# A batched matmul with 24 KB weight runs, half-lane ends and the x cast moved to VectorE

## The chip, the cores and the metric

One core of one Trainium2 chip runs the kernel; the chip's other cores are idle. The metric is the device time of one execution in microseconds (us). A timed comparison is several runs of a kernel and of the kernel before on the same chip. Ratios are the mean time of one kernel's fast runs over that of the other's of the same rounds, so they are not quite the ratio of the medians that are quoted.

## The reference

128 independent products, each [256 x 512] times [512 x 384] in fp32:

```python
b1, b2, m, k, n = 8, 16, 256, 512, 384
x      = randn(b1, b2, m, k)      # 67 MB
weight = randn(b1, b2, k, n)      # 101 MB
out    = np.matmul(x, weight)     # 50 MB
```

## The kernel before

Four products make a group, so there are 32 groups. A group's x lies in 128 partitions of eight rows (16 KB runs), its output the same way (12 KB runs). The kernel casts x and weights to bf16 and transposes x on TensorE. Then it multiplies, with each strip of 32 output partitions serving one of the four products. A lane is one of a tile's partitions, 128 of them in most tiles (the x cast's form on the page is 128x1024); PSUM is where the code puts TensorE's results, the tiles `pt` and `po`. A packet is one partition's run: the page counts 18,864, which is 128 for each of the 131 transfers and 16 of 4 bytes for its semaphore, 9 ns each. In the code the semaphores count work done, and `wait_ge` holds an engine until a count is reached (SyncE is held 269.5 us by casts of weights, in the waits view).

```python
G = 4; R = 8; T = 4; D = 2; S = 2; HP = 64      # group of 4, two pairs, halves of 64 lanes
XS, WS, OS = 2, 4, 4                            # buffers of x, of weight pairs, of output
BS, TS, WBS = 1, 2, 8                           # x in bf16, x transposed, weights in bf16

def load(e, t, U, s):                           # SyncE: two weight pairs, then x
    for d in range(G // D):
        e.wait_ge(w_cast, ...)                  # this buffer's old weights are cast
        e.dma_start(w_sb[slot][:], ...)         # 128 runs of 12 KB
    e.wait_ge(x_cast, ...)
    e.dma_start(x_sb[s % XS][:], ...)           # 128 runs of 16 KB

def prepare(e, t, U, s):                        # VectorE
    for d in range(G // D):
        ...                                     # wait for the pair
        for a in range(D):
            for h in range(S):
                e.tensor_copy(w_bf[...][h*HP:(h+1)*HP], w_sb[slot][a*HP:(a+1)*HP, ...])
    for q in range(T):
        e.wait_ge(t_made, ...)
        e.tensor_copy(x_t[...], pt[...])        # transposed x, PSUM to SBUF

def multiply(e, t, U, s):                       # TensorE: transposes of group n, then its products
    for q in range(T):
        e.wait_ge(x_cast, ...)
        ...                                     # 4 transposes
    e.wait_ge(w_cast, ...)
    for q in range(T):
        ...                                     # 32 matmuls
# ScalarE: four casts of x (cast_x), then four copies of the products to out_sb (copy_out)
# SyncE's loop: load group n, then store group n - 4
... (cut)
```

Of the kernel before, what the change touches and what calls it, by code (L numbers as in the profile page):

```python
# [12 lines left out]
def kernel(  # L13
# [6 lines left out]
    nc = tc.nc  # L20
    P = 128

    b1, b2, M, K = x.shape
    _, _, _, N = weight.shape
    B = b1 * b2
    KO = K // P

    x_rows = x.rearrange("b1 b2 m k -> (b1 b2 m) k")
    w_rows = weight.rearrange("b1 b2 k n -> (b1 b2 k) n")
    o_rows = out.rearrange("b1 b2 m n -> (b1 b2 m) n")  # L30

    fp32 = mybir.dt.float32
    bf16 = mybir.dt.bfloat16
# [3 lines left out]



    G = 4  # L40
    C = P // G
    R = G * M // P
    T = R // 2
    D = 2
    S = 2
    HP = P // D
    NG = B // G

    XS, WS, OS = 2, 2 * G // D, 4
    BS, TS, WBS = 1, 2, 2 * G  # L50
    PT, PO = 4, 2

    LAG = 4

    ctx.enter_context(tc.tile_critical(no_gpsimd_drain=True))  # L55

    def sbuf(name, shape, dtype, n):
        return [
            ctx.enter_context(nc.sbuf_tensor(f"{name}{s}", shape, dtype)) for s in range(n)
        ]  # L60
# [6 lines left out]
    def sems(name, n):  # L67
        return [tc.alloc_semaphore(f"{name}{s}") for s in range(n)]
# [2 lines left out]
    identity = sbuf("identity", [P, P], fp32, 1)[0]  # L71
    x_sb = sbuf("x_sb", [P, R, K], fp32, XS)

    x_bf = sbuf("x_bf", [P, R, S, HP, KO], bf16, BS)
    x_t = sbuf("x_t", [P, R, KO // 2, P, 2], bf16, TS)
    w_sb = sbuf("w_sb", [P, S * KO, N], fp32, WS)
    w_bf = sbuf("w_bf", [P, KO, N], bf16, WBS)
    out_sb = sbuf("out_sb", [P, R, N], fp32, OS)
    pt = psum("pt", [P, 2, KO // 2, P], fp32, PT)
# [2 lines left out]



    id_done, x_cast, w_cast, t_made, t_copied, p_made, o_copied = (
        sems(name, 1)[0]
        for name in (
            "id_done", "x_cast", "w_cast", "t_made", "t_copied", "p_made", "o_copied"
        )
    )  # L90
    x_in, w_in, o_out = sems("x_in", XS), sems("w_in", WS), sems("o_out", OS)


    BIAS = 8


    def load(e, t, U, s):
        n = t * U + s
        for d in range(G // D):
            slot = (s * (G // D) + d) % WS  # L100
            if not isinstance(n, int) or n >= 2:
                e.wait_ge(w_cast, n * (G * S) + ((d + 1) * D * S - 2 * G * S))
            e.dma_start(  # L103
                w_sb[slot][:],
                w_rows[bass.ds(n * (G * K) + d * (D * K), D * K)].rearrange(
                    "(p k) n -> p k n", k=S * KO
                ),
            ).then_inc(w_in[slot], 16)
        if not isinstance(n, int) or n >= XS:
            e.wait_ge(x_cast, n * T + (1 - XS) * T)  # L110
        e.dma_start(  # L111
            x_sb[s % XS][:],
            x_rows[bass.ds(n * (G * M), G * M)].rearrange("(p r) k -> p r k", r=R),
        ).then_inc(x_in[s % XS], 16)

    def store(e, t, U, s, pieces=1):
        n = t * U + s
        dram = o_rows[bass.ds(n * (G * M), G * M)].rearrange("(p r) n -> p r n", r=R)
        for q in range(pieces):
            rows = slice(q * R // pieces, (q + 1) * R // pieces)  # L120
            e.wait_ge(o_copied, n * T + ((q + 1) * T // pieces + BIAS))
            e.dma_start(out=dram[:, rows], in_=out_sb[s % OS][:, rows]).then_inc(
                o_out[s % OS], 16
            )

    def cast_x(e, t, U, s, q):
        n = t * U + s
        if q == 0:
            e.wait_ge(x_in[s % XS], (t * (U // XS) + s // XS) * 16 + 16)
        e.wait_ge(t_made, n * T + (q + 1 - T + BIAS))  # L130
        rows = slice(2 * q, 2 * q + 2)
        e.copy(  # L132
            out=x_bf[s % BS][:, rows],
            in_=x_sb[s % XS][:, rows].rearrange("p r (q s c) -> p r s q c", s=S, c=KO),
        ).then_inc(x_cast, 1)

    def prepare(e, t, U, s):
        n = t * U + s
        e.wait_ge(p_made, n * T + (BIAS - T))
        for d in range(G // D):  # L140
            slot = (s * (G // D) + d) % WS
            e.wait_ge(
                w_in[slot], (t * (U * G // D // WS) + s * G // D // WS) * 16 + 16
            )
            for a in range(D):
                for h in range(S):
                    e.tensor_copy(  # L147
                        out=w_bf[(s * G + d * D + a) % WBS][h * HP : (h + 1) * HP],
                        in_=w_sb[slot][a * HP : (a + 1) * HP, h * KO : (h + 1) * KO, :],
                    ).then_inc(w_cast, 1)  # L150
        for q in range(T):
            e.wait_ge(t_made, n * T + (q + 1 + BIAS))
            e.tensor_copy(  # L153
                out=x_t[s % TS][:, 2 * q : 2 * q + 2],
                in_=pt[(s * T + q) % PT][:].bitcast(bf16),
            ).then_inc(t_copied, 1)

    def multiply(e, t, U, s):
        n = t * U + s
        words = x_bf[s % BS][:].rearrange("p r s q c -> p r (s q c)").bitcast(fp32)  # L160
        for q in range(T):
            e.wait_ge(x_cast, n * T + (q + 1))
            e.wait_ge(t_copied, n * T + (q + 1 - PT + BIAS))
            for rr in range(2):
                for h in range(KO // 2):
                    ins = e.transpose(  # L166
                        pt[(s * T + q) % PT][:, rr, h, :],
                        words[:, 2 * q + rr, h :: KO // 2],
                        identity[:],
                    )  # L170
            ins.then_inc(t_made, 1)
        e.wait_ge(w_cast, n * (G * S) + G * S)
        for q in range(T):
            e.wait_ge(t_copied, n * T + (q + 1 + BIAS))
            e.wait_ge(o_copied, n * T + (q + 1 - PO + BIAS))
            for rr in range(2):
                for ko in range(KO):
                    for i in range(G):
                        mine = slice(i * C, (i + 1) * C)
                        ins = e.matmul(  # L180
                            po[(s * T + q) % PO][mine, rr, :N],
                            x_t[s % TS][:, 2 * q + rr, ko // 2, mine, ko % 2],
                            w_bf[(s * G + i) % WBS][:, ko, :],
                            start=(ko == 0),
                            stop=(ko == KO - 1),
                        )
            ins.then_inc(p_made, 1)

    def copy_out(e, t, U, s, q):
        n = t * U + s  # L190
        if q == 0:
            e.wait_ge(o_out[s % OS], (t * (U // OS) + s // OS) * 16 + 16)
        e.wait_ge(p_made, n * T + (q + 1 + BIAS))  # L193
        e.copy(  # L194
            out=out_sb[s % OS][:, 2 * q : 2 * q + 2, :],
            in_=po[(s * T + q) % PO][:, :, :N],
        ).then_inc(o_copied, 1)
# [7 lines left out]
    def on_sync(e):  # L205
        U = OS
        for n in range(LAG):
            load(e, 0, NG, n)
        rounds = (NG - LAG) // U
        with e.Fori(0, rounds) as t:  # L210
            for s in range(U):
                load(e, t, U, LAG + s)
                store(e, t, U, s)
        for n in range(rounds * U, NG):
            if n + LAG < NG:
                load(e, 0, NG, n + LAG)
            store(e, 0, NG, n, T if n == NG - 1 else 1)
        for s in range(OS):
            e.wait_ge(o_out[s], 16 + 16 * (NG // OS + (T - 1 if s == (NG - 1) % OS else 0)))

    def on_vector(e):
        U = 2
        e.sem_inc(t_copied, BIAS)
        with e.Fori(0, NG // U) as t:
            for s in range(U):
                prepare(e, t, U, s)

    def on_tensor(e):
        U = 2
        e.sem_inc(t_made, BIAS)  # L230
        e.sem_inc(p_made, BIAS)
        e.wait_ge(id_done, 2)

        pe = mybir.EngineType.PE
        with nc.Fori(0, NG // U, engines=OrderedEngineSet([pe]), head_slot={pe: 0}) as t:
            for s in range(U):
                multiply(e, t, U, s)

    def on_scalar(e):
        U = OS  # L240
        e.sem_inc(o_copied, BIAS)
        for s in range(OS):
            e.sem_inc(o_out[s], 16)

        with e.Fori(0, NG // U) as t:
            for s in range(U):
                for q in range(T):
                    cast_x(e, t, U, s, q)
                for q in range(T):
                    copy_out(e, t, U, s, q)  # L250

    on_gpsimd(nc.gpsimd)
    on_sync(nc.sync)
    on_vector(nc.vector)
    on_tensor(nc.tensor)
    on_scalar(nc.scalar)


# [28 lines left out]
```

## Time and profile before

| what | value | where |
|---|---|---|
| time | 518.8 us, median of 3, 518.78 to 518.82 | timed runs |
| moved | 218.1 MB at 429 GB/s in mid-run | queue line, windows |
| busy, VectorE / TensorE / ScalarE | 64% / 59% / 46% | page, part 1 |

How to read it: each kernel's page gives the busy time of every engine, the DMA line in 40 slices (9 means 90% or more), the chain that ended last and the groups of instructions. A row of the windows view gives the stretch, its length, the busy time of the engines asked for, TensorE's granted clock, the share of the sixteen DMA engines' time, and GB/s. The lines themselves stand in the prediction.

### The profile page before, as it was taken

The numbers are of one execution on the slowest core, as the hardware profiler recorded it, in microseconds if no ns is written. First come the engines' busy times: TensorE is split into PE (matmuls) and PEld (weight loads), VectorE is DVE, ScalarE is ACT, GpSimd is POOL, SyncE is SP. The second block draws the span as 40 slices with busy tenths as digits, with TensorE's granted clock in tenths as the row PEclk, the third lists the DMA queues.
The fourth block names the chain that finished last, engine by engine and source line by source line (L and its number), as shares of the span: only waits on it lengthen the run. The fifth ranks groups of instructions, "written<-read, shape, count | busy, mean of one in ns | idle before, by whom it ended". The sixth has DMA issues, their size and how long they took to land.

```text
span 517.2 us, 11523 instructions
## 1 busy us (share of the span) xinstructions
PE 306.6 (59%) x4608; PEld 200.6 (39%) x4608; DVE 332.8 (64%) x384; ACT 236.7 (46%) x264; POOL 0.7 (0%) x6
## 2 busy tenths in 40 slices
PE   0478776556665457645577554776446765467752
PEld 0345444334443334433344332444324443244431
DVE  3698875667556676556675566855658656676550
ACT  0465564443644436435355354454444544544441
POOL 0000000000000000000000000000000000000000
PEclk9998877878777887878777778877788877778777
DMA  8999999999999999999999999999999999999996
GB/s 340 430 423 424 424 432 426 429 428 430 432 427 427 427 428 432 429 427 430 426 431 431 426 429 430 427 432 427 427 429 429 427 433 425 430 428 430 429 428 251
DMA packets 18869, 218.18 MB, mean 422 GB/s; under 512 B 2096, under 2 KB 2096, under 8 KB 2608
## 3 DMA queue, kind: packets, MB, share of 16 engines
q1 hardware_dynamic: 18864, 218.11, 99.3%
q8 instruction: 3, 0.05, 0.0%
q14 instruction: 2, 0.02, 0.0%
HBM read 167.77 MB, written 50.33 MB: 422 GB/s over the span
## 4 chain that ended last, share of the span: by engine, by line
DMA 81%; ACT 10%; PE 4%; issue 3%; ACTq 0%; SPq 0%
DMA x_sb<-in_x_dram 81%; ACT x_bf L132 9%; PE po L180 2%; PE pt L166 1%; ACTq L130 0%; ACT out_sb L194 0%; SPq L111 0%; SPq L103 0%; ACT L132 0%; ACTq L193 0%; SPq L282 0%; SPq L55 0%
## 5 line engine op out<-in xcount | busy, mean ns | idle before, releaser
L147 DVE CAST w_bf<-w_sb 64x1536 bf16<-64x1536 f32 x256 | 244.4, 955 | 47.2 <-DMA w_sb<-in_weight_dram 38.5
L166 PE MATMUL pt<-identity,x_bf 128*128 128x128 f32 x512 | 123.7, 425 | 199.3 <-ACT x_bf L132 199.1
L180 PE MATMUL po<-w_bf,x_t 128*32 128x384 bf16 x4096 | 185.1, 342 | 1.0 <-issue 1.0
L166 PEld LDWEIGHTS pt<-identity,x_bf 128*128 128x128 f32 x512 | 91.8, 216 | 232.1 <-issue 218.3
L194 ACT COPY out_sb<-po 128x768 f32<-128x768 f32 x128 | 102.2, 798 | 147.2 <-PE po L180 147.2
L153 DVE COPY x_t<-pt 128x1024 bf16<-128x1024 bf16 x128 | 88.4, 691 | 122.3 <-PE pt L166 121.8
L132 ACT CAST x_bf<-x_sb 128x1024 bf16<-128x1024 f32 x128 | 124.4, 1042 | 80.9 <-DMA x_sb<-in_x_dram 80.8
L180 PEld LDWEIGHTS po<-w_bf,x_t 128*32 128x32 bf16 x4096 | 108.8, 101 | 73.8 <-issue 14.2
L132 ACT ACT_TABLE_LOAD x8 | 10.3, 1283 | 42.9 <-DMA x_sb<-in_x_dram 42.9
masks.py:199 POOL TENSOR_SCALAR_AFFINE_SELECT identity<-identity 128x128 f32<-128x128 f32 x1 | 0.3, 292 | 0.2 <-POOL identity L200 0.2
L200 POOL MEMSET identity<- 128x128 f32 x1 | 0.2, 204 | 0.5 <-SPq L55 0.5
L271 POOL MEMSET const-bfloat16-1.0<- 128x1 bf16 x1 | 0.1, 101 | 0.0
L271 POOL MEMSET const-uint8-127<- 128x1 uint8 x1 | 0.1, 101 | 0.0
L271 POOL MEMSET const-float32-0.0<- 128x1 f32 x1 | 0.1, 98 | 0.2 <-issue 0.2
L271 POOL MEMSET const-float32-1.0<- 128x1 f32 x1 | 0.1, 98 | 0.0
## 6 DMA issues: line engine op xcount, KB each, us to landing
w_sb<-in_weight_dram SPq DMA_DIRECT2D x64, 1536.0 KB, 27.5
x_sb<-in_x_dram SPq DMA_DIRECT2D x32, 2048.0 KB, 27.5
out_dram<-out_sb SPq DMA_DIRECT2D x31, 1536.0 KB, 30.7
out_dram<-out_sb SPq DMA_DIRECT2D x4, 384.0 KB, 5.9
```

Source lines behind the costliest of these rows:

```text
L132: e.copy(out=x_bf[s % BS][:, rows], in_=x_sb[s % XS][:, rows].rearrange("p r (q s c) -> p r s q c", s=S, c=KO),).then_inc(x_cast, 1)
L147: e.tensor_copy(out=w_bf[(s * G + d * D + a) % WBS][h * HP : (h + 1) * HP], in_=w_sb[slot][a * HP : (a + 1) * HP, h * KO : (h + 1) * KO, : ...
L153: e.tensor_copy(out=x_t[s % TS][:, 2 * q : 2 * q + 2], in_=pt[(s * T + q) % PT][:].bitcast(bf16),).then_inc(t_copied, 1)
L166: ins = e.transpose(pt[(s * T + q) % PT][:, rr, h, :], words[:, 2 * q + rr, h :: KO // 2], identity[:],)
L180: ins = e.matmul(po[(s * T + q) % PO][mine, rr, :N], x_t[s % TS][:, 2 * q + rr, ko // 2, mine, ko % 2], w_bf[(s * G + i) % WBS][:, ko, :], ...
L194: e.copy(out=out_sb[s % OS][:, 2 * q : 2 * q + 2, :], in_=po[(s * T + q) % PO][:, :, :N],).then_inc(o_copied, 1)
L200: e.memset(identity[:], 0.0).then_inc(id_done, 1)
L271: nc = _bacc.Bacc("TRN2", target_bir_lowering=False, num_devices=1)
```

## The change

It lengthens a weight load from two transfers with runs of 12 KB per partition to one with runs of 24 KB. A run of 24 KB puts a product's weights into 32 partitions, so each cast covers 32 lanes and there are 16 of them, not 8. VectorE cannot take them all: 16 and four x casts would last over the 15.9 us in which a group's bytes move. So ScalarE gets five, VectorE eleven. In exchange VectorE casts x and ScalarE copies the transposed x out of PSUM. VectorE casts the next group's x between its weight casts, and TensorE transposes it ahead of this group's products. SyncE's order changes too: it issues x, the store, then weights, where it issued weights, x, then the store. The first four groups and the last two stay with 12 KB halves and casts of 64 lanes.

```diff
-    D = 2
-    S = 2
+    SH, SL = 2, 4                     # rows of weights per partition in short and long groups
-    XS, WS, OS = 2, 2 * G // D, 4
+    XS, WS, OS = 2, 2, 4
+    CA = 5                            # weight casts of ScalarE
+    CV = G * SL - CA                  # of VectorE
+    XV = 8                            # of these, ahead of the next x
+    def is_short(n):
+        return isinstance(n, int) and (n < LAG or n >= NG - 2)
+    def load_w(e, t, U, s):           # waits for both engines' casts, then one transfer (short: two)
...
     def on_tensor(e):
+        transpose(e, 0, NG, 0)
-            for s in range(U):
-                multiply(e, t, U, s)
+            transpose(e, t, U, 1)
+            multiply(e, t, U, 0)
+            with e.If(t < NG // U - 1):
+                transpose(e, t, U, 2)
+            multiply(e, t, U, 1)
...
+        def step(t, U, s):            # VectorE
+            cast_w(e, t, U, s, range(XV))
+            next_x(t, U, s)
+            cast_w(e, t, U, s, range(XV, CV), False)
...
+        def step(t, U, s):            # ScalarE
+            evacuate(e, t, U, s + 1)
+            for q in range(T):
+                copy_out(e, t, U, s, q)
+                if q > 0:             # long groups: one cast, one, then three
+                    cast_w(e, t, U, s + 1, ...)
... (cut: semaphores, SyncE's order x, store, weights, unrolled ends)
```

## The prediction

> **What bounds the kernel now.** I read the page from the top: busy shares first, then the line of the DMA engines, then the chain that ended last, then the waits of the queue that issues the transfers, and last the two ends in windows. The busy shares, the slices and the queues:
>
> ```profile
> span 517.2 us, 11523 instructions
> ...
> PE 306.6 (59%) x4608; PEld 200.6 (39%) x4608; DVE 332.8 (64%) x384; ACT 236.7 (46%) x264; POOL 0.7 (0%) x6
> ...
> DMA  8999999999999999999999999999999999999996
> GB/s 340 430 423 424 424 432 426 429 428 430 432 427 427 427 428 432 429 427 430 426 431 431 426 429 430 427 432 427 427 429 429 427 433 425 430 428 430 429 428 251
> ...
> q1 hardware_dynamic: 18864, 218.11, 99.3%
> ```
>
> No engine is above 64%, but the one DMA queue fills 99.3% of sixteen engines' span, and between the first and the last slice nothing dips. The chain agrees, and so do the groups of instructions:
>
> ```profile
> DMA 81%; ACT 10%; PE 4%; issue 3%; ACTq 0%; SPq 0%
> ...
> L147 DVE CAST w_bf<-w_sb 64x1536 bf16<-64x1536 f32 x256 | 244.4, 955 | 47.2 <-DMA w_sb<-in_weight_dram 38.5
> ...
> L194 ACT COPY out_sb<-po 128x768 f32<-128x768 f32 x128 | 102.2, 798 | 147.2 <-PE po L180 147.2
> L153 DVE COPY x_t<-pt 128x1024 bf16<-128x1024 bf16 x128 | 88.4, 691 | 122.3 <-PE pt L166 121.8
> L132 ACT CAST x_bf<-x_sb 128x1024 bf16<-128x1024 f32 x128 | 124.4, 1042 | 80.9 <-DMA x_sb<-in_x_dram 80.8
> ```
>
> The casts wait for data from the DMA; the idle time of ScalarE and TensorE follows from that. The transfers' own waits need care:
>
> ```profile
> SPq L103 <- DVE w_bf L147: 269.5, 60, 8.6
> SPq L111 <- ACT x_bf L132: 122.5, 30, 5.6
> ```
>
> SyncE waits 269.5 + 122.5 us for buffers to come free. By itself that looks like "slow casts hold back the loads". It does not: a load takes 27.5 us from issue to landing (the page's part on DMA issues), far longer than its bytes need, so it spends most of this behind other transfers. The buffers are late, the DMA engines are not empty. The windows show how full they are:
>
> ```profile
> core 0: us, PE busy (x) PEld busy (x) DVE busy (x) ACT busy (x) POOL busy (x), PEclk, DMA share, GB/s
> ...
> 60.00:450.00 390.00, 237.01 (x3580) 154.81 (x3572) 257.50 (x297) 182.04 (x203) 0.00 (x0) 0.79 1.01 429
> ...
> 500.00:505.00 5.00, 5.00 (x96) 3.52 (x99) 2.02 (x3) 2.02 (x3) 0.00 (x0) 0.88 1.01 428
> 505.00:510.00 5.00, 1.87 (x48) 1.01 (x40) 0.00 (x0) 1.72 (x3) 0.00 (x0) 1.00 0.98 409
> 510.00:517.20 7.20, 0.00 (x0) 0.00 (x0) 0.00 (x0) 0.00 (x0) 0.00 (x0) 0.60 0.31 124
> ```
>
> A share of 1.01 (packet records overlap by some ns) at 429 GB/s over 390 us, and still 428 GB/s at 505 us, where the last group is being multiplied. So the time is bytes over rate plus two short ends. In the trace's packet records the first packet starts at 2.0 us and all engines are full until about 511 us; then they run out one after another, the last at 515.4 us. One group of four products moves 2.097 MB of x, 3.146 MB of weights and 1.573 MB of output, 6.816 MB, which at 429 GB/s is 15.9 us; 32 of them are 509 us, and the remaining 8 us of the span are the ends.
>
> [...] between 60 and 450 us a packet of 12,288 B lasts 461.3 ns on average and one of 16,384 B 614.5 ns. The 4,096 B more cost 153.1 ns; three times that is 459.4 ns, so the fixed part of a 12 KB packet is about 2 ns.
>
> [...]
>
> **The change part by part.** Bytes: none removed.
>
> (1) Runs. 26 of 32 groups load their weights as one transfer of 24 KB per partition in place of two of 12 KB; the first four and last two keep halves of 12 KB. Each long group saves 128 packets, 26 x 128 = 3328, at 2 ns each over 16 engines: 0.4 us. It also saves one transfer's 16 semaphore packets of 9 ns, one per engine: 26 x 9 ns = 0.2 us. Together 0.6 us, 0.1% of the time, all on the path. That is the entire direct gain I can find.
>
> (2) VectorE. It loses the PSUM copies of the transposed x (4 x 0.69 = 2.8 us per group) and gets the x cast: [...] about 0.69 us, four of them 2.8 us. [...] Weight casts go from 8 of 64 lanes to 16 of 32 lanes; [...] each still costs 955 ns (in the timeline eight in a row take 7.86 us, 0.98 each). VectorE keeps 11: 11 x 0.98 = 10.8 us. Sum 13.6 us per long group against 10.6 before.
>
> (3) ScalarE. It loses the x casts (4.2 us) and gets four PSUM copies of 1024 (about 1.04 us each, 4.2 us) and five weight casts of 1536 elements: [...] 1.47 us each, 7.3 us. With the output copies (4 x 0.80 = 3.2 us) that is 14.7 us per long group against 7.4 before. Whole-run busy time should be near 410 us on VectorE and 425 us on ScalarE.
>
> (4) Order on TensorE. Transposes of group n+1 go before the products of n. Now about 4 us of transposes stand between the x cast and the products; this takes them out of that chain. It shortens a group's latency, which is not what ends the kernel: worth 0.
>
> (5) Buffers. Still two of x and two of weights, so a buffer goes round in 31.8 us (two periods). Weights are now held until all casts are through, roughly 13.6 us after landing if VectorE starts at the landing, which leaves 31.8 - 13.6 = about 18 us from issue to landing, in place of 27.5. The x load stands behind that weight load on the same issuing engine; it would be issued just after it and take about 23 us to land. A load's own bytes need 4.9 to 7.3 us, so there would still be over 10 us of transfers ahead of each new one. I expect no gap.
>
> (6) Ends. The last loads are followed by the stores of groups 27 to 31, 3.7 us each. After the last weights land (halves let VectorE cast the first while the second comes) come about 4 us of casts, 5.4 us of products and a copy, some 11 us, while four older stores keep the engines busy for 4 x 3.7 = 14.7 us. So the last store should be ready in time and the tail be as before; likewise the head, where the first load is issued at once in both. Worth 0 +- 1 us.
>
> Sum: 518.8 - 0.6 = 518.2 us.
>
> **The rivals.** First, ScalarE or VectorE becomes the bound. For: 14.7 and 13.6 us of a 15.9 us period are 92% and 86%[...], and each waits on the other through TensorE. [...] Against: the rate of the weight cast and two weight buffers of slack.
>
> Second, weight buffers held too long starve the DMA queue. For: long loads free a buffer only as a whole, and only when the slower of two engines is done. Against: the 10 us computed in (5). If it did happen, a 1 us gap per group would make 544 us, so even a small gap shows.
>
> Third, longer runs lift the transfer rate itself[...]. For: the engines end 4 us apart, so the slowest sets the end. [...] Against: 16 KB packets move at 26.66 bytes per ns and 12 KB ones at 26.63; nothing rises with size. [...]
>
> **Range and chances.** The centre is 518.2 us. Repeats differ by 0.04 us; the ends can move by 1 us either way, and a mild third rival could take 1 or 2 us. The first two rivals lie above, with some 7% of passing 529 us or more. Range 516.3 to 520.4 us. Faster by over 2%[...]: 1%. Within 2%: 92%. Slower: 7%.
>
> **What would show each step.** Right: DMA share still 1.01 at 428 to 430 GB/s in mid-run; packets about 15,100; weights landing about 18 us after issue and x later; weight casts 955 ns on VectorE and 1.47 us on ScalarE; x cast on VectorE near 0.69 us; TensorE's transposes ahead of the products with the time unmoved. Wrong: a digit of 8 or less in the DMA line in mid-run, [...] ScalarE busy over 90% in the middle with the loads waiting for its casts, a 24 KB packet well off 921 ns, or a tail in which the engines stand empty before the last store is issued.

The sum came to 518.8 - 0.4 - 0.2 = 518.2 us: 2 ns a packet and 9 ns a semaphore packet both come from the packet records of the kernel before. The 0.69 us of an x cast on VectorE and the 1.47 us of a weight cast on ScalarE went into the 13.6 and 14.7 us a group and into point (5); when the forecast was made no trace showed them, and the run after does: 688 and 1468 ns. It also shows that a cast of 32 lanes lasts as long as one of 64 (951 and 955 ns on VectorE), and a PSUM copy of 1024 on ScalarE took 1025 ns. The small size of the third rival and the 1% for faster stand as estimates; that the rate had no more room was not shown.

## The result, and the profile after

518.6 us (median of 4 runs, 518.19 to 518.67) against 518.8 us; ratio 0.9994, interval 0.9977 to 1.0012. Same time, 0.4 us from the predicted 518.2 us and inside the range. From the page of the changed kernel:

```profile
span 516.8 us, 11572 instructions
...
PE 315.2 (61%) x4608; PEld 225.4 (44%) x4608; DVE 397.7 (77%) x462; ACT 410.3 (79%) x387; POOL 0.7 (0%) x6
...
q1 hardware_dynamic: 15120, 218.11, 99.0%
...
DMA 57%; DVE 29%; issue 9%; PE 1%; SPq 1%; DVEq 1%; ACT 0%
...
L162 DVE CAST w_bf<-w_sb 32x1536 bf16<-32x1536 f32 x286 | 271.9, 951 | 81.6 <-DMA w_sb<-in_weight_dram 73.5
...
L162 ACT CAST w_bf<-w_sb 32x1536 bf16<-32x1536 f32 x130 | 190.9, 1468 | 6.0 <-DMA w_sb<-in_weight_dram 2.8
...
L188 ACT COPY x_t<-pt 128x1024 bf16<-128x1024 bf16 x128 | 120.3, 1025 | 22.1 <-PE pt L201 21.5
L149 DVE CAST x_bf<-x_sb 128x1024 bf16<-128x1024 f32 x128 | 80.0, 688 | 12.4 <-DMA x_sb<-in_x_dram 11.5
...
w_sb<-in_weight_dram SPq DMA_DIRECT2D x26, 3072.0 KB, 18.1
x_sb<-in_x_dram SPq DMA_DIRECT2D x32, 2048.0 KB, 22.3
```

Every duration is near its forecast: weight casts 951 and 1468 ns, the x cast 688 ns. ScalarE has gone from 237 to 410 us, and yet the queue is as full. The chain now gives 29% to VectorE. That is no sign of a VectorE bound: the chain walks from a landing back to the cast that released the buffer. It can't see that the transfer had others ahead of it. The last figures of the two transfer lines show that it had: 18.1 and 22.3 us from issue to landing. The windows in mid-run (columns as in the prediction) show the rate up:

```profile
60.00:450.00 390.00, 244.55 (x3480) 174.80 (x3484) 312.64 (x363) 342.05 (x316) 0.00 (x0) 0.76 1.01 431
```

431 against 429 GB/s over nearly 500 us should be worth 2 us. The end of the kernels shows where that goes. First the kernel before, in windows of 1 us, with GpSimd as the only engine column (it is idle):

```profile
core 0: us, POOL busy (x), PEclk, DMA share, GB/s
...
510.00:511.00 1.00, 0.00 (x0) 1.00 1.02 412
511.00:512.00 1.00, 0.00 (x0) 0.70 0.67 270
512.00:513.00 1.00, 0.00 (x0) 0.50 0.28 111
513.00:514.00 1.00, 0.00 (x0) 0.50 0.16 65
514.00:515.00 1.00, 0.00 (x0) 0.50 0.07 28
```

And the changed kernel:

```profile
510.00:511.00 1.00, 0.00 (x0) 1.00 0.45 181
511.00:512.00 1.00, 0.00 (x0) 0.55 0.22 89
512.00:513.00 1.00, 0.00 (x0) 0.50 0.06 25
513.00:514.00 1.00, 0.00 (x0) 0.50 0.07 28
514.00:515.00 1.00, 0.00 (x0) 0.50 0.05 22
```

A share of 0.06 is one engine of sixteen. Most engines end over 1 us earlier after the change, and then one engine works alone for nearly 3 us.

The packet records can be taken further. They carry no engine number. But divided over sixteen chains, nearly every packet of the kernels before and after starts 3 to 4 ns before the end of another, and so each packet can be given to the engine whose previous one had just ended. Of 15,000 to 19,000 packets a few dozen at most (5 to 41) fit with a gap of over 60 ns; that is the quality of what follows. The end of the last store on each engine, and the profiled execution's own time:

| kernel (names as in the next section) | fastest engine | mean | last engine | time | time less last |
|---|---|---|---|---|---|
| before | 511.0 | 512.2 | 515.4 | 518.98 | 3.6 |
| changed | 509.6 | 510.8 | 514.9 | 518.58 | 3.7 |
| changed, again | 509.6 | 510.7 | 514.6 | 518.31 | 3.7 |
| split | 511.5 | 512.6 | 516.1 | 519.77 | 3.6 |
| order_only | 511.5 | 512.7 | 517.2 | 520.87 | 3.7 |

The time is the last engine's end plus 3.6 to 3.7 us in all of them; over the mean engine it lies anything from 6.8 to 8.2 us. The change brings the mean engine forward by 1.4 us, the last one by 0.5 us.

### The profile page after: what moved, and what is told of

Same layout as the page of the kernel before. It is cut to its first block, busy times and chain, and to the rows that moved or that the text cites. A ratio compares the mean times of both kernels' runs of the same rounds, so it can differ in the third digit from the quotient of the medians.

```text
span 516.8 us, 11572 instructions
## 1 busy us (share of the span) xinstructions
PE 315.2 (61%) x4608; PEld 225.4 (44%) x4608; DVE 397.7 (77%) x462; ACT 410.3 (79%) x387; POOL 0.7 (0%) x6
## 4 chain that ended last, share of the span: by engine, by line
DMA 57%; DVE 29%; issue 9%; PE 1%; SPq 1%; DVEq 1%; ACT 0%
DMA w_sb<-in_weight_dram 57%; DVE w_bf L162 20%; DVE x_bf L149 5%; DVE w_bf L178 4%; PE po L219 1%; SPq L125 0%; DVEq L288 0%; SPq L108 0%; DVEq L158 0%; ACT out_sb L233 0%; SPq L120 0%; DVEq L146 0%; DVEq L172 0%; SPq L372 0%; SPq L60 0%
## 5 line engine op out<-in xcount | busy, mean ns | idle before, releaser
L162 DVE CAST w_bf<-w_sb 32x1536 bf16<-32x1536 f32 x286 | 271.9, 951 | 81.6 <-DMA w_sb<-in_weight_dram 73.5
L219 PE MATMUL po<-w_bf,x_t 128*32 128x384 bf16 x4096 | 200.6, 359 | 38.3 <-DVE w_bf L162 21.0
L201 PE MATMUL pt<-identity,x_bf 128*128 128x128 f32 x512 | 115.0, 415 | 152.2 <-DVE x_bf L149 152.2
L162 ACT CAST w_bf<-w_sb 32x1536 bf16<-32x1536 f32 x130 | 190.9, 1468 | 6.0 <-DMA w_sb<-in_weight_dram 2.8
L201 PEld LDWEIGHTS pt<-identity,x_bf 128*128 128x128 f32 x512 | 103.4, 224 | 164.1 <-issue 163.8
L219 PEld LDWEIGHTS po<-w_bf,x_t 128*32 128x32 bf16 x4096 | 122.0, 106 | 115.9 <-issue 40.7
L188 ACT COPY x_t<-pt 128x1024 bf16<-128x1024 bf16 x128 | 120.3, 1025 | 22.1 <-PE pt L201 21.5
L149 DVE CAST x_bf<-x_sb 128x1024 bf16<-128x1024 f32 x128 | 80.0, 688 | 12.4 <-DMA x_sb<-in_x_dram 11.5
L178 DVE CAST w_bf<-w_sb 64x1536 bf16<-64x1536 f32 x48 | 45.9, 955 | 8.3 <-DMA w_sb<-in_weight_dram 7.0
## 6 DMA issues: line engine op xcount, KB each, us to landing
w_sb<-in_weight_dram SPq DMA_DIRECT2D x26, 3072.0 KB, 18.1
x_sb<-in_x_dram SPq DMA_DIRECT2D x32, 2048.0 KB, 22.3
```

The costliest lines, as they stand in the source:

```text
L149: e.tensor_copy(out=x_bf[s % BS][:, rows].rearrange("p r (s q c) -> p r s q c", s=S, c=KO), in_=x_sb[s % XS][:, rows].rearrange("p r (q s ...
L162: copy(out=w_bf[(s * G + i) % WBS][h * C : (h + 1) * C], in_=w_sb[s % WS][i * C : (i + 1) * C, h * KO : (h + 1) * KO, :],).then_inc(w_vcas ...
L178: e.tensor_copy(out=w_bf[(n * G + d * SH + a) % WBS][h * p : (h + 1) * p], in_=w_sb[n % WS][a * p : (a + 1) * p, r : r + KO, :],).then_inc ...
L188: e.copy(out=x_t[s % TS][:, 2 * q : 2 * q + 2], in_=pt[(s * T + q) % PT][:].bitcast(bf16),).then_inc(t_copied, 1)
L201: ins = e.transpose(pt[(s * T + q) % PT][:, rr, h, :], words[:, 2 * q + rr, h :: KO // 2], identity[:],)
L219: ins = e.matmul(po[(s * T + q) % PO][mine, rr, :N], x_t[s % TS][:, 2 * q + rr, ko // 2, mine, ko % 2], w_bf[(s * G + i) % WBS][:, ko, :], ...
```

## The experiments

Theory A: the DMA engine that finishes last sets the end, and the compute engines are hidden. Rivals: the order of casts and transposes is what matters; the lag of the last engine is chance, or all engines share the end. All kernels were correct except the three thin ones. The kernel before, run beside them, had medians of 518.47 to 518.55 us.

**after_again: the changed kernel once more, as yardstick.** No edit.

> The changed kernel once more, as the yardstick for the other runs of this call. Theory A (the DMA engine that finishes last sets the end, and all else is hidden): 518.2 to 518.7 us again, packets of 24 KB at 912 ns, and in the last 4 us of transfers a DMA share near 0.06, one engine of sixteen. Theory B (the lag of that engine is chance): the tail looks different from run to run and the times spread by 1 us or more.

518.31 us (518.19 to 518.71), ratio 0.9999. The tail has the same form, with shares of 0.07, 0.06 and 0.04 from 512 to 515 us, and the times spread by 0.5 us: the lag comes again and is not chance from run to run.

**split: run length alone taken back.**

```diff
+        if not is_short(n):
+            for h in range(2):
+                half = slice(h * 2 * KO, (h + 1) * 2 * KO)
+                e.dma_start(w_sb[s % WS][:, half, :], rows[:, half, :]).then_inc(w_in[s % WS], 16)
+            return
... (cut: rows, and the casts' wait for both transfers)
```

> The changed kernel, but each 24 KB run of weights fetched as two runs of 12 KB into the same place, two transfers in place of one; all casts, waits and orders stay. Theory A: 24 KB packets save about 10 ns of packet time per pair, 208 pairs per engine, so packet time per engine rises by about 2 us back to 513.7, and the time rises by 0.4 to 2 us, to 519 to 520.5 us. If the change's gain came from the order of the casts (rival): no rise, 518.5 us. By the prediction's 2 ns per packet: plus 0.6 us.

519.77 us (519.65 to 519.96), ratio 1.0025. So run length (with one transfer in place of two) is worth 1.46 us, and the rest of the change, by subtraction, costs 1.3 us against the kernel before: two effects of opposite sign make the "same". Neither size is exact, as the edit also moves a fetch of instructions to another engine (see pad). In the packet records two 12 KB packets take 2 x 461.6 ns and a 24 KB packet 912.2 ns, 11 ns less; mean packet time per engine falls from 514.2 to 511.6 us. The rate is that of the kernel before again:

```profile
60.00:450.00 390.00, 0.00 (x0) 0.77 1.01 429
```

**order_only: the order and the exchange of engines alone.** Every group in halves, eight casts of 64 lanes on VectorE, none on ScalarE. SyncE's new order (x, store, weights), weight buffers that come free only as a whole, and the unrolled ends stay in it as well.

```diff
-        return isinstance(n, int) and (n < LAG or n >= NG - 2)
+        return True
-                if q == 0 and short:
-                    e.sem_inc(w_acast, CA)
... (cut: the other waits for ScalarE's casts, indices of cast_short)
```

> All groups as two halves of 12 KB cast in half lanes by VectorE alone (8 casts), so the order on TensorE and the exchange of x cast and PSUM copy between VectorE and ScalarE are all that is left of the change. Theory A: the order is worth 0; 518.8 us within 0.5. Rival (transposes ahead of the products free buffers earlier and close gaps in the transfers): faster than the kernel before by over 1 us. DMA share in mid-run 1.01 at 428 to 429 GB/s under A.

520.87 us (520.15 to 521.25), ratio 1.0045: slower by 2.4 us, which no theory expected. The rival's gap closing did not show; the mid-run share is 1.01 at 429 GB/s, as A had it. Mean engine: 512.7 us, only 0.5 later than before. The difference is in the last one:

```profile
515.00:516.00 1.00, 0.00 (x0) 0.50 0.07 28
516.00:517.00 1.00, 0.00 (x0) 0.50 0.06 25
```

Still one engine at work at 517 us. In the chains followed through groups 12 to 22, one and the same engine, the one that ends last, loses 114 to 134 ns on the median engine in every store here. In the changed kernel the slowest loses 110 to 138 ns in about every third store and 24 to 46 ns in the others; in the kernel before 0 to 82 ns. Why this changes is open, and so is which part of the edit does it: TensorE's order, SyncE's order and the place of the code are not told apart here. A fetch of 8 KB of instructions at 95 us also falls on this engine, which goes from 0.06 us ahead of the median engine at 60 us to 0.6 us behind at 100 us.

**last15: the last store laid on fifteen engines.**

```diff
-            e.dma_start(out=dram[:, rows], in_=out_sb[s % OS][:, rows]).then_inc(o_out[s % OS], 16)
+            cuts = (slice(0, 120), slice(120, 128)) if pieces > 1 else (slice(0, P),)
+            for c in cuts:
+                e.dma_start(out=dram[c, rows], in_=out_sb[s % OS][c, rows]).then_inc(...)
... (cut: the final wait's count)
```

The author took it that 120 rows would use fifteen engines and 8 rows eight. The trace agrees with the counts: 28 packets more, which is four times 15 + 8 semaphore packets in place of 16. Which engines they are it does not show.

> The changed kernel, with each of the four pieces of the last store cut into partitions 0 to 119 and 120 to 127, which should leave one of the sixteen DMA engines without any work in that store (if 120 rows are spread over fifteen engines). If the engine that finishes last is the one left out: it ends up to 3.7 us earlier, the next one lags about 2.5 us less than it, so the time falls by 1.5 to 3 us to 515.5 to 517 us. If it is another engine: plus 0.2 to 1 us. If the end is set by something else than an engine's own backlog: no change.

520.38 us (519.23 to 521.15), ratio 1.0033: slower by 2.1 us than the changed kernel, more than any of the cases. In the trace the last engine writes nine packets per piece, so it has work in both cuts: the one left out was not the slow one. The four packets added there are only 0.5 us. Its lag had not grown (4.2 us on the median engine after the store of group 29, 4.6 in the changed kernel), but in the next store two of its 12 KB packets took 785 and 1874 ns in place of 460, 1.7 us in all. No kernel of the table above has a 12 KB packet over 0.7 us after 500 us; what starts these is open. No gain, and it does not tell which engine it is.

**one_store: the last output in one transfer.**

```diff
-            store(e, 0, NG, n, T if n == NG - 1 else 1)
+            store(e, 0, NG, n)
... (cut: the final wait's count)
```

> The changed kernel, with the output of the last group stored in one transfer in place of four, so it can only be issued after the last copy, near 506.6 us[...]. In the changed kernel the fastest DMA engine was through with its backlog at 505.8 us and the slowest at 511.1 us. Theory A (the slowest engine sets the end): the fast engines stand empty for 2 to 3 us and it costs nothing; the time stays within 0.5 us of 518.3, perhaps 0.1 less because 12 KB packets replace 3 KB ones. Rival (the last store follows a chain of work, or all engines share the end): plus 1.5 to 3 us.

518.38 us (518.03 to 518.82), ratio 0.9998. The windows show the price, and that it isn't paid:

```profile
505.00:510.00 5.00, 0.00 (x0) 1.00 0.84 356
510.00:511.00 1.00, 0.00 (x0) 0.52 0.93 393
511.00:512.00 1.00, 0.00 (x0) 0.50 0.18 74
512.00:513.00 1.00, 0.00 (x0) 0.50 0.06 25
```

From 505 to 510 us the share is 0.84 where the changed kernel has 0.96: the fast engines wait for the store, up to 1.6 us, whose first packet starts at 507.4 us, 0.8 us after its issue at 506.6. (The 2 to 3 us expected rested on a longer delay, which no run shows.) But from 512 us on it is again one engine, and the time is the same. This is the cleanest support for theory A.

**long_ends: the last two groups as long ones.**

```diff
-        return isinstance(n, int) and (n < LAG or n >= NG - 2)
+        return isinstance(n, int) and n < LAG
```

> The changed kernel with the last two groups as long ones too (24 KB, casts of 32 lanes shared by VectorE and ScalarE). The last weights then wait for 11 casts of VectorE, 10.8 us, and 5.4 us of products after landing: some 3 to 5 us later than with half-lane ends. By the prediction's part on the ends there are 14.7 us of older stores to hide 17 us, so plus about 2 us. Theory A: the slowest engine has its backlog until 511 us, which hides most of it: 0 to plus 1 us, less 0.1 us for two more groups of 24 KB packets.

524.88 us (523.56 to 525.5), ratio 1.0127: 6.6 us slower than after_again, three times what the prediction's arithmetic gives. The timeline (start, duration, engine) names what it left out:

```profile
494.05 13.71 DVE L162 CAST w_bf<-w_sb 32x1536 bf16<-32x1536 f32 x14
...
505.34 4.45 ACT L162 CAST w_bf<-w_sb 32x1536 bf16<-32x1536 f32 x3
...
510.13 7.01 PE L219 MATMUL po<-w_bf,x_t 128*32 128x384 bf16 x128 [7.33 <-ACT w_bf L162]
```

VectorE is through at 507.8 us; the products start at 510.1, after ScalarE's last three casts, which stand behind the output copies of group 30. The transfers run dry meanwhile (the share is 0.03 from 510 to 511 us). So the half-lane ends are worth 6.6 us: without them this change would be a loss.

**fetch8: the kernel before, with a loop on TensorE four times as long.**

```diff
     def on_tensor(e):
-        U = 2
+        U = 8
```

The trace of the kernel before has three packets of 16 KB in the queue that the page calls instruction, 1.0 to 1.1 us each. In the chains, three engines fall back at just these moments and stay behind; the two that can be read cleanly go from 0.77 to 2.34 and from 0.59 to 2.17 us behind the fastest, about 1.6 us for a fetch.

> The kernel before with TensorE's loop unrolled to 8 groups a turn in place of 2: same work, four times the code in the loop. In the trace a fetch of 16 KB of instructions takes 1.1 us on one DMA engine, and that engine then runs 2 us behind the others. Theory A: if the longer loop makes many more fetches[...], the engines lose 1 to 2 us per fetch, spread over those they fall on, and the time rises by 3 us if spread evenly and by tens of us if on one engine. If fetches cost the transfers nothing: 518.5 us. If the loop still fits and nothing is fetched: no change and nothing learnt.

524.52 us (524.45 to 525.9), ratio 1.0125. The queue that fetches instructions, which stood at 3 packets before:

```profile
q8 instruction: 43, 0.70, 0.6%
```

The count of fetches behind the 3 us expected is cut, as no trace before showed the size of the code; the run has 40 more. 40 fetches at 1.6 us, spread evenly over 16 engines, would be 4 us (an estimate from these two traces); 6.0 us were measured. In the chains of the kernel before a fetch puts back an engine that moves data, by about 1.6 us. How much of the 6 us is the engines' and how much the tail's, which is thinner here, was not separated.

**thin_before, thin_after, thin_order: the floor of the engines.** From the fifth group on, each load moves one row per partition in place of eight (weights: one of eight or sixteen), stores one always; casts, transposes, products and waits stay.

```diff
-            x_sb[s % XS][:],
+            x_sb[s % XS][:, :r],      # r = R for the first four groups, then 1
...                                    # the same for weights; stores one row of eight
```

> A wrong result on purpose: from the fifth group on, each load and each store moves one row in place of eight (and stores always one), with all waits, casts, transposes and products as they are, so what is left is the time of the engines. The kernel before chains x casts (3.9 us), the last transposes and PSUM copy (1.2), the products (5.4 to 6.3) and the last output copy (0.9) from group to group: about 12 us a group, 28 x 12 plus some 50 us for the first four full groups = 385 us.

> The same for the changed kernel. ScalarE is the busiest: 3.8 (PSUM copies) + 3.2 (output copies) + 7.3 us (five weight casts) = 14.3 us for a long group by the changed kernel's own profile, and VectorE 13.2. If the engines' busy time sets the floor, 26 x 14.5 plus some 60 us for the ends = 435 us; so the change would have raised the floor over the 385 us of the kernel before, the opposite of what it is meant for. Rival (transposes ahead of the products shorten the chain, so the floor falls): under 385 us. If the floor is near 510 us, the compute engines were the bound beside the DMA engines after all.

> The same for the kernel with the order and exchange of engines alone (halves everywhere, no weight casts on ScalarE). VectorE has 8 x 0.98 + 4 x 0.63 = 10.4 us a group, TensorE 3.6 + 5.4 to 6.3, ScalarE 7. Floor 28 x 10.4 plus some 50 us = 340 us: transposes ahead of the products would shorten what bounds the engines, by 1 to 2 us a group against the kernel before.

405.18, 472.87 and 358.50 us: in the order expected, each 5 to 9% over its number. Mid-run windows (columns PE, PEld, DVE, ACT, POOL) of the first:

```profile
100.00:380.00 280.00, 217.93 (x3324) 139.78 (x3324) 242.47 (x282) 173.44 (x195) 0.00 (x0) 0.85 0.23 71
```

of the second:

```profile
100.00:440.00 340.00, 217.63 (x3302) 142.16 (x3303) 299.94 (x348) 322.34 (x299) 0.00 (x0) 0.80 0.14 44
```

and of the third:

```profile
100.00:340.00 240.00, 192.51 (x3328) 134.25 (x3328) 234.23 (x281) 159.79 (x186) 0.00 (x0) 0.97 0.26 81
```

VectorE runs 12 instructions a group in the first and third and 15 in the second. So a group takes 280 / (282 / 12) = 11.9 us, 340 / (348 / 15) = 14.7 us and 240 / (281 / 12) = 10.2 us. All lie below the 15.9 us of the transfers, so none of them shows. The order with the exchange of engines does what it is meant for, 1.7 us a group off the engines' own period, though TensorE's granted clock differs as well (0.85, 0.80 and 0.97 in these windows), and how much of the 1.7 us is the clock's was not separated. The casts of 32 lanes then add 4.4 us, with ScalarE busy for 322 of 340 us. What hides behind the transfers has shrunk from 4.0 to 1.2 us a group.

**pad: more code in SyncE's loop.**

```diff
+        if not isinstance(n, int):
+            for _ in range(6):
+                e.sem_inc(spare, 1)
... (cut: the spare semaphore)
```

> The changed kernel, with six increments of a spare semaphore, which nobody reads, ahead of each weight load in SyncE's loop: no work, only more code there. In both traces of the changed kernel a fetch of 8 KB of instructions at 422 us falls on the engine that is last anyway and puts it back by 1 us; in the kernel with split runs, whose loop on SyncE is longer, that fetch comes at 90 us and falls on another engine. Theory A: here too the fetch moves away from 422 us, the last engine gains about 1 us and the time is 517.3 us, within 0.4. If the fetch stays at 422 us: 518.3 us and nothing learnt. If it moves and the time stays at 518.3 us, the late fetch is not what holds back the last engine.

518.08 us (518.03 to 518.41), ratio 0.9991, interval 0.9977 to 1.0005. The fetch moved from 422 to 88 us as expected, but the time fell by 0.2 us and not by 1. A miss. In the chains, one more engine has fallen 2 us behind by 130 us, and it is the one that ends last, 5.3 us after the fastest as in the changed kernel: the fetch at 88 us falls on it (0.4 us behind the median engine at 60 us, 1.4 at 100 us). So the fetch moved in time but not to another engine, and the run does not tell what the time would be without it. In split the fetch near 90 us falls on an engine that doesn't end last, so part of the differences between the kernels may lie in where a fetch falls; no run takes that apart.

**store_last: the store behind the weights in SyncE's loop.**

```diff
                 load_x(e, t, U, LAG + s)
-                store(e, t, U, s)
                 load_w(e, t, U, LAG + s)
+                store(e, t, U, s)
```

> The changed kernel with SyncE's loop issuing x, weights, store in place of x, store, weights. In the traces the engine that ends last loses its time mostly in the stores: in the kernel with the order alone about 120 ns more than the other engines in every store, in the changed kernel in every third, in the kernel before 20 to 80 ns. If that loss hangs on what is moved beside or just ahead of a store, it changes here, and the end moves with it, by up to 2 us either way, while the mean engine ends within 0.2 us of 510.7. If the loss belongs to the engine and the store alone: 518.3 us again. The order of casts and products is as in the changed kernel, so a theory that puts the time there expects no change.

532.76 us (three runs near 531 and three above 534), ratio 1.0281: 14 us slower, far outside the 2 us expected. The rate in slices of 13 us:

```profile
GB/s 337 426 424 431 423 443 424 430 425 427 429 440 429 427 429 434 426 435 434 430 425 429 429 434 436 426 423 420 395 416 389 397 391 429 429 426 409 299 430 156
```

It is as ever until about 370 us, then falls to 389 to 416 GB/s for five slices with the engines still 90% busy. In the packet records 24 KB packets of up to 2.6 us appear there, 1.7 us over their usual 912 ns, while the casts keep their durations. Packet time per engine is 519.5 us in place of 511.6, 8 of the 13 us by which this profiled execution is longer. The rest is the slices near the end (the share is 0.85 at 303 GB/s from 490 to 500 us) and a last engine that ends 6 us after the mean. What starts the long packets is open. It does say that with equal bytes and equal casts the order of the transfers can cost more than any other single edit told here, so SyncE's new order is a rival to TensorE's order for what the change costs.

No version beat both kernels beyond noise: pad, the lowest, is 0.09% under the kernel before, inside its interval.

## Why the prediction was right or wrong, point by point

- **The bound** (bytes over rate, then two short ends): right, as one_store and the three floors show. But "the ends" was too coarse: 3 us of the last 5 are one engine of sixteen. The prediction saw that the engines end 4 us apart, and used it only in its third rival.
- **(1) Runs, 0.6 us**: this step failed in size. Taking the run length back cost 1.46 us. The fixed part of 2 ns per packet came from the step between 12 and 16 KB packets. But the 16 KB packet is itself longer than the line through the others: from 12 to 24 KB 12,288 B cost 912.5 - 461.2 = 451.3 ns, so by these two the fixed part is 9.9 ns, and 16 KB should take 611.6 ns where 614.3 were measured. Two points, one of them odd, gave the wrong slope. So the trace did not bear out the small cost per packet that the prediction took from it. Packet time per engine fell by 2.6 us (514.2 to 511.6), and 1.46 us of it reached the time.
- **(2) VectorE and (3) ScalarE**: right. The x cast, with its runs of four elements, took 688 ns against the 0.69 us told, and a cast of 32 lanes lasts as long as one of 64 (951 and 955 ns). Busy times of 398 and 410 us were 3 to 4% under the 410 and 425 told, as neighbouring instructions overlap: four x casts take 2.50 us in the timeline, not 2.8.
- **(4) Order on TensorE, worth 0**: true of the buffers and the waits, not of the time. Order and exchange, with SyncE's order, cost 2.4 us, and everything but the run length 1.3 us; that TensorE's order is the cause was not shown. The prediction gives SyncE's order of x, store and weights no term at all. The gain that was too small and the cost that was left out nearly cancel; that the centre was only 0.4 us off is partly luck.
- **(5) Buffers, 18 and 23 us to landing**: right, 18.1 and 22.3.
- **(6) Ends, 0 +- 1 us**: held, but the margin was worked out for VectorE alone. For whole-lane ends that would have missed ScalarE, as long_ends showed.
- **Rivals**: the first two did not come about. The floor of 14.7 us is nearer to 15.9 than the kernel before was, so the first was worth its place. The third was half right: longer runs do lift the rate (431 against 429 GB/s; why was not tested), and the last engine's lag takes part of it back.

What stays open: which engine is last, why it loses time in stores, which part of the change (TensorE's order, SyncE's order or where the code's fetches fall) alters that loss, and what starts the long packets of store_last and last15.

## What to carry to other kernels

Where the DMA engines are full from end to end, a better compute schedule bought nothing here, and a change that leans on the compute engines only spent the room beneath the transfers: measure that floor with thin transfers before and after. Look at the last few microseconds engine by engine: here the mean engine ended 1.4 us earlier, the slowest 0.5, and the time of these two executions fell by 0.4: a gain in the mean rate reached the time only as far as the slowest engine shared it. And a "same" can be two effects of opposite sign, which one run that takes back a single part shows.
